# Shifting the wide weight tiles of a two-layer decoder trunk by 64 bytes

## The chip, the core and the metric

The kernel runs on one core of a Trainium2 chip. The metric is the device time of one execution in microseconds. Three runs of the kernel before took 2226.98, 2228.97 and 2231.87 us; the median is 2228.97 us.

## The reference, cut to what matters

Two layers over 512 tokens of width 1024, all in float32. Each layer is a half-step SwiGLU FFN, a token mixer (retention in layer 0, attention with forget gates in layer 1), a second half-step FFN, and a gated per-layer embedding; RMSNorm stands ahead of each, and at the end.

```python
def swiglu(x, w_in, w_out):
    g, u = jnp.split(x @ w_in, 2, axis=-1)
    return (jax.nn.silu(g) * u) @ w_out

for i in range(DEPTH):                       # DEPTH = 2
    h = h + 0.5 * swiglu(rmsnorm(h, nw[0]), ffn_w_in[i, 0], ffn_w_out[i, 0])
    hn = rmsnorm(h, nw[1])
    h = h + (retention(hn, ...) if i == 0 else forgetting_attention(hn, ...))
    h = h + 0.5 * swiglu(rmsnorm(h, nw[2]), ffn_w_in[i, 1], ffn_w_out[i, 1])
    gate = jax.nn.sigmoid(rmsnorm(h, nw[3]) @ ple_w_gate[i])
    h = h + gate * (p[i] @ ple_w_proj[i])
return rmsnorm(h, final_norm_w)
```

`D_MODEL` is 1024 and `D_FF` is 2816.

## The kernel before

**Precision.** Every float32 operand is split into a high part, rounded to the matmul's input format, and a low part, the rest. A product is three matmuls: high by high, high by low, low by high. `mm3` (lines 312 to 314) issues them; line 493 does the same for the FFN's products.

**Layout.** Tokens lie along the free axis. Activations are held in "units" of 128 partitions by 512 columns (pools `ua`, `ub`, `uc`, `ud`, names `unit_a` to `unit_d`). In nearly all matmuls a 128x128 piece of a weight tile is the stationary operand, which a weight load brings into TensorE ahead of each matmul, and a unit is the moving operand: all 512 columns (lines 312 to 314) or one half of 256 columns (lines 493 and 524). In the value projections of the two mixers (lines 678 to 680) it is the other way round: a unit is stationary and 512 columns of a wide weight tile move.

**Weights.** A wide weight tile (name `w8`, shown as `w`) holds the high and the low part of 1024 columns, 8192 bytes in each partition. Three of them rotate in the pool `wpool`. They are filled in the order of a plan, two ahead of use: a DMA on SP's queue into `wraw`, a rounding copy on ScalarE (line 82), and a subtraction on VectorE or GpSimd (line 83), or, for some, a DMA on GpSimd's queue that adds into the tile (line 122).

**FFN.** Of the 22 column blocks of an FFN, two (`plain`, line 524) are computed directly, in 192 matmuls of 256 columns. The other 20 (`start`, `one`, `two`, `three`) use a form of Strassen's method: seven products of 12 matmuls of 256 columns each, line 493. Two of the seven take their weights from the wide tile, 24 matmuls; the other five take them from tiles that the FFN's own pool holds, `s12` and `s34` (sums of weight blocks, shown as `s`) and `a12` (shown as `a`), 60 matmuls. After each of three chunks of blocks the output projection (`out_blocks`) runs 512-column matmuls on wide tiles.

**Where the tiles lie.** Pools are placed one behind the other in each partition. In the built program of before, the units, `wraw`, the three wide tiles of `wpool` and `tmp` begin at 32 modulo 128 bytes. The FFN's `s` and `a` tiles begin at 96 modulo 128, and at 224 modulo 256. In the last stage (`ple` of layer 1, two passes of 256 tokens) five further wide tiles come from a pool `wkept`, which begins at 96 modulo 128; and eight units of `unit_b` hold weights there. All pieces of a tile that a matmul takes lie at multiples of 512 bytes from its beginning, so they share its residue.

**Counts in the program.** Matmuls whose stationary operand lies in `wpool`: 4104 of 512 columns, 2832 of 256 columns (1920 on line 493, 768 on line 524, 144 in the last stage). With a wide tile as the moving operand: 576 of 512 columns. With `s` or `a` stationary: 4800 of 256 columns. With `wkept` stationary: 240 of 256 columns.

**Order.** TensorE's order is the order of the code. The other engines are ordered by the scheduler.

Of the kernel before, what the change touches and what calls it, by code (L numbers as in the profile page):

```python
# [11 lines left out]
F32 = mybir.dt.float32  # L12
# [5 lines left out]
P = 128  # L18
# [169 lines left out]
def trunk(ctx, tc, a):  # L188
    nc = tc.nc
# [6 lines left out]
    uc = ctx.enter_context(tc.tile_pool(name="uc", bufs=4))  # L196
    ud = ctx.enter_context(tc.tile_pool(name="ud", bufs=16))
    wraw = ctx.enter_context(tc.tile_pool(name="wraw", bufs=4))
    wpool = ctx.enter_context(tc.tile_pool(name="wpool", bufs=LOOKAHEAD + 1))
    tmp = ctx.enter_context(tc.tile_pool(name="tmp", bufs=7))  # L200
    stat = ctx.enter_context(tc.tile_pool(name="stat", bufs=1))
    psum = ctx.enter_context(tc.tile_pool(name="psum", bufs=8, space=bass.MemoryType.PSUM))
# [1126 lines left out]
```

## Time and profile before

| | |
|---|---|
| runs | 2226.98, 2228.97, 2231.87 us |
| span of the profiled execution | 2230.5 us |
| granted TensorE clock, mean | 0.987 |
| matmuls | 13525 |
| DMA | 272.33 MB, mean 122 GB/s |

The profile is of one execution whose span, from the first to the last instruction, was 2230.5 us; no other time is given for that execution, and the span lies between the lowest and the highest of the runs. Starts are given in us from the first instruction. The records of matmuls overlap: a matmul's duration covers its way through the array, and the next one starts before it ends. How much time a matmul takes away from the rest is therefore the distance from its start to the next start, called the pitch below. It is read by subtracting two starts and dividing by the count of matmuls between them.

### The profile page before, as it was taken

The page shows a single profiled execution, that of the slowest core. Times are in us where ns is not written, and L with a number is a line of the kernel's source. Part 1 is how long each engine was busy: PE and PEld are TensorE (multiplying, and loading weights), DVE is VectorE, ACT ScalarE, POOL GpSimd, SP SyncE. Part 2 cuts the span into 40 slices and gives each one's busy share as a digit, 9 for nine tenths or more (in the row PEclk, how much of TensorE's full clock was granted, in tenths as well). Part 3 has the DMA queues.
Part 4 walks back from the last instruction along what each step waited for, and adds up shares of the span by engine and source line. Part 5 has one row for each costly group of instructions (what it writes and reads, how often), then busy time and mean ns, then how long its engine had stood idle before and what let it go on. Part 6 is the DMA issues. An engine that isn't in the chain of part 4 may idle for free.

```text
span 2230.5 us, 34455 instructions
## 1 busy us (share of the span) xinstructions
PE 2154.5 (97%) x13525; PEld 1937.5 (87%) x13525; DVE 1447.1 (65%) x2631; ACT 1212.3 (54%) x2037; POOL 450.7 (20%) x352
## 2 busy tenths in 40 slices
PE   7999999999999999999997999999999999999998
PEld 7999997888888798989876989898788888999987
DVE  8686776352542776767746677675675686777764
ACT  7565553433233663735555646364786775555543
POOL 0010003444444010101110001012334200110154
PEclk9999999999999999999998999999999999999999
DMA  5465563232222254746464457373622244655631
GB/s 176 113 163 150 138 161 95 81 99 76 88 83 76 85 137 119 170 133 152 129 151 117 114 136 182 113 167 103 153 91 87 69 116 112 159 158 137 152 104 39
DMA packets 86755, 272.33 MB, mean 122 GB/s; under 512 B 9520, under 2 KB 13104, under 8 KB 86592
## 3 DMA queue, kind: packets, MB, share of 16 engines
q1 hardware_dynamic: 63328, 209.78, 28.7%
q0 software_dynamic: 22032, 59.25, 15.9%
q8 instruction: 106, 1.74, 0.3%
q10 hardware_dynamic: 1232, 1.09, 0.1%
q14 instruction: 57, 0.47, 0.1%
HBM read 267.96 MB, written 2.13 MB: 121 GB/s over the span
## 4 chain that ended last, share of the span: by engine, by line
PE 80%; DVE 7%; ACT 6%; DMA 4%; issue 3%; POOL 0%; SPq 0%; DVEq 0%; ACTq 0%; POOLq 0%
PE bank L493 29%; PE bank L314 14%; PE bank L312 13%; PE bank L313 13%; PE bank L524 3%; DMA wraw<-in_ffn_w_in 3%; PE bank L678 2%; PE bank L679 2%; PE bank L680 2%; DVE w L83 1%; DMA w<-in_ple_gate 1%; DVE sums L151 1%; ACT p L982 1%; ACT w L82 1%; DVE tlo L303 1%
## 5 line engine op out<-in xcount | busy, mean ns | idle before, releaser
L82 ACT CAST w<-wraw 128x1024 fp32r<-128x1024 f32 (+1 forms) x232 | 235.1, 1021 | 431.0 <-PE bank L314 252.6
L314 PE MATMUL bank<-unit_a,w 128*128 128x512 f32 x736 | 288.9, 393 | 12.7 <-DMA w<-in_ple_gate 8.4
L312 PE MATMUL bank<-unit_a,w 128*128 128x512 f32 x736 | 289.8, 394 | 1.9 <-ACT w L82 1.6
L313 PE MATMUL bank<-unit_a,w 128*128 128x512 f32 x736 | 287.9, 391 | 0.2 <-DVE unit_a L303 0.2
L82 ACT CAST s<-sums 128x512 fp32r<-128x512 f32 x320 | 191.2, 617 | 155.3 <-DVE sums L151 106.6
L314 PE MATMUL bank<-unit_d,w 128*128 128x512 f32 (+1 forms) x712 | 268.1, 377 | 4.6 <-DVE w L83 4.6
L312 PE MATMUL bank<-unit_d,w 128*128 128x512 f32 (+1 forms) x712 | 269.2, 378 | 3.2 <-ACT w L82 1.6
L313 PE MATMUL bank<-unit_d,w 128*128 128x512 f32 (+1 forms) x712 | 268.3, 377 | 1.8 <-DVE unit_d L303 1.8
L83 DVE TENSOR_TENSOR s<-sums,s 128x512 fp32r<-128x512 f32 x320 | 213.7, 686 | 81.4 <-ACT s L82 80.4
L83 POOL TENSOR_TENSOR w<-wraw,w 128x1024 fp32r<-128x1024 f32 x83 | 202.6, 2445 | 233.5 <-ACT w L82 223.4
L122 POOL DMA_DIRECT2D a<-in_ffn_w_in x80 | 70.1, 876 | 651.4 <-ACT a L121 444.8
L83 DVE TENSOR_TENSOR w<-wraw,w 128x1024 fp32r<-128x1024 f32 (+1 forms) x149 | 175.8, 1185 | 28.3 <-ACT w L82 27.7
L493 PE MATMUL bank<-unit_b,s 128*128 128x256 f32 x880 | 185.9, 278 | 0.0
L493 PE MATMUL bank<-unit_d,s 128*128 128x256 f32 x1140 | 179.2, 277 | 0.0
L314 PEld LDWEIGHTS bank<-unit_a,w 128*128 128x128 f32 x736 | 138.8, 189 | 45.5 <-DMA w<-in_ple_gate 10.1
L493 PE MATMUL bank<-unit_a,s 128*128 128x256 f32 x1260 | 176.1, 277 | 1.9 <-ACT unit_a L376 1.1
L585 DVE SCALAR_TENSOR_TENSOR tmp<-bank,rows 128x512 f32<-128x512 f32 x96 | 66.0, 689 | 165.3 <-PE bank L314 164.0
L312 PEld LDWEIGHTS bank<-unit_a,w 128*128 128x128 f32 x736 | 139.0, 189 | 32.4 <-ACT w L82 3.5
L313 PEld LDWEIGHTS bank<-unit_a,w 128*128 128x128 f32 x736 | 139.0, 189 | 28.8 <-DVE unit_a L303 0.5
L493 PEld LDWEIGHTS bank<-unit_a,s 128*128 128x128 f32 x1260 | 158.8, 188 | 2.7 <-ACT unit_a L376 1.6
L314 PEld LDWEIGHTS bank<-unit_d,w 128*128 128x128 f32 x712 | 134.4, 189 | 30.5 <-DVE w L83 6.6
L312 PEld LDWEIGHTS bank<-unit_d,w 128*128 128x128 f32 x712 | 134.5, 189 | 30.3 <-ACT w L82 3.3
(270 smaller groups left out, 4801.1 us busy)
## 6 DMA issues: line engine op xcount, KB each, us to landing
wraw<-in_ffn_w_in SPq DMA_DIRECT2D x174, 512.0 KB, 4.3
wraw<-in_ffn_w_out SPq DMA_DIRECT2D x64, 512.0 KB, 4.7
w<-in_ffn_w_in POOLq DMA_DIRECT2D x58, 512.0 KB, 5.5
a<-in_ffn_w_in POOLq DMA_DIRECT2D x80, 256.0 KB, 6.2
wraw<-in_ffn_w_out SPq DMA_DIRECT2D x32, 384.0 KB, 3.7
wraw<-in_ret_qk SPq DMA_DIRECT2D x16, 512.0 KB, 3.5
wraw<-in_ret_v SPq DMA_DIRECT2D x16, 512.0 KB, 3.6
wraw<-in_ret_g SPq DMA_DIRECT2D x16, 512.0 KB, 3.5
```

What stands on the lines that cost most here:

```text
L82: self.nc.scalar.copy(hi, raw)
L83: self.low.tensor_tensor(out=lo, in0=raw, in1=hi.bitcast(F32), op=ALU.subtract)
L122: self.nc.gpsimd.dma_start(out=lo, in_=src, accum_op=ALU.add)
L312: nc.tensor.matmul(out, wh, xh, start=first, stop=False)
L313: nc.tensor.matmul(out, wh, xl, start=False, stop=False)
L314: nc.tensor.matmul(out, wl, xh, start=False, stop=last)
L493: add = lambda w, x, start, stop: nc.tensor.matmul(out, w, x, start=start, stop=stop, skip_group_check=True)
L524: nc.tensor.matmul(o[:, HALVES[t]], x[:, ks], y, start=k == t == q == 0, stop=k == KB - 1 and q == 2, skip_group_check=True,)
L585: nc.vector.scalar_tensor_tensor(out=t1, in0=o, scalar=-0.5, in1=n.r, op0=ALU.mult, op1=ALU.mult)
L678: nc.tensor.matmul(os[t], xh, wh[:, js], start=k == 0, stop=False)
L679: nc.tensor.matmul(os[t], xh, wl[:, js], start=False, stop=False)
L680: nc.tensor.matmul(os[t], xl, wh[:, js], start=False, stop=k == KB - 1)
```

## The change

Two tiles of 128 partitions by 16 float32, 64 bytes in each partition, are allocated: one ahead of `wpool` and one behind it. GpSimd fills each with zeros once, and nothing reads them. The wide tiles then begin at 96 modulo 128. What is allocated behind the second gap is moved by 128 bytes, so `tmp`, the statistics and the pools of the stages keep their residue modulo 128; their residue modulo 256 changes (`s` and `a` from 224 to 96). Everything ahead of `wpool` stays.

```diff
     wraw = ctx.enter_context(tc.tile_pool(name="wraw", bufs=4))
+    nc.gpsimd.memset(ctx.enter_context(tc.tile_pool(name="gap0", bufs=1)).tile([P, 16], F32, name="gap0"), 0.0)
     wpool = ctx.enter_context(tc.tile_pool(name="wpool", bufs=LOOKAHEAD + 1))
+    nc.gpsimd.memset(ctx.enter_context(tc.tile_pool(name="gap1", bufs=1)).tile([P, 16], F32, name="gap1"), 0.0)
     tmp = ctx.enter_context(tc.tile_pool(name="tmp", bufs=7))
```

On GpSimd the program of before begins like this, up to the identity matrix that the transposes use:

```order
L1319 MEMSET const-uint8-127 128x1
L1325 UNCONDITIONAL_BRANCH
masks.py:197 MEMSET ident 128x128
masks.py:199 ISA
masks.py:199 AFFINE_SELECT ident<-ident 128x128
L122 DMA a_434<-in_ffn_w_in 128x512
```

The changed program has the two fills at the same place:

```order
L1321 MEMSET const-uint8-127 128x1
L1327 UNCONDITIONAL_BRANCH
L199 MEMSET gap_81 128x16
L201 MEMSET gap_89 128x16
masks.py:197 MEMSET ident 128x128
masks.py:199 ISA
masks.py:199 AFFINE_SELECT ident<-ident 128x128
L122 DMA a_444<-in_ffn_w_in 128x512
```

Two short instructions more stand ahead of the identity matrix. On the other four queues, TensorE's, VectorE's, ScalarE's and SP's, the instructions and their order are the same as before; only line numbers, buffer numbers and addresses differ.

## The prediction

> **What bounds the kernel now.** I began with the page's busy times and its chain of work that ended last.
>
> ```profile
> PE 2154.5 (97%) x13525; PEld 1937.5 (87%) x13525; DVE 1447.1 (65%) x2631; ACT 1212.3 (54%) x2037; POOL 450.7 (20%) x352
> PE 80%; DVE 7%; ACT 6%; DMA 4%; issue 3%; POOL 0%; SPq 0%; DVEq 0%; ACTq 0%; POOLq 0%
> ```
>
> TensorE (PE) is busy for 97% of the span, and four fifths of the chain are its own matmuls. No other engine is near its limit. The chain in order of time shows an FFN chunk as one piece, and the window view how much room the others have there:
>
> ```profile
> 884.61 77.44 PE bank L493 x672
> ...
> 1027.92 5.29 DMA wraw<-in_ffn_w_in
> ```
> ```profile
> 900.00:960.00 60.00, 60.00 (x523) 60.00 (x523) 48.40 (x88) 44.14 (x77) 9.60 (x11) 1.00 0.76 188
> ```
>
> Columns of the second: PE, PEld, DVE, ACT and POOL busy, granted clock, DMA share, GB/s. Inside a chunk PE has no gap, VectorE is at 48.4/60 = 81% and DMA at 0.76: what changes the pitch of matmuls there changes the time. From 1027.92 on the chain passes through weight loads, and a faster PE would only wait longer.
>
> Nothing but addresses changes, so the question is whether the pitch depends on them. I looked at the order of time of TensorE, where the columns are start, duration, line, operands and count:
>
> ```profile
> 65.10 2.88 PE L493 MATMUL bank<-unit_a,s 128*128 128x256 f32 x24
> 67.82 1.60 PE L493 MATMUL bank<-unit_a,w 128*128 128x256 f32 x12
> 69.26 0.73 PE L493 MATMUL bank<-unit_b,s 128*128 128x256 f32 x5
> ```
>
> 24 matmuls with weights in `s` (96 modulo 128) take 67.82 - 65.10 = 2.72 us, a pitch of **113.3 ns**; 12 with weights in `w` (32) take 1.44 us, **120.0 ns**. Width, line and moving units are the same. The chunk agrees to the last digit: 672 matmuls are 8 blocks of 60 and 24, 480 x 113.3 + 192 x 120.0 = 77.4 us. So weights 64 bytes away from the residue of the moving operand seem to cost 6.7 ns less. Two further views say that this is not all.
>
> First, the 512-column matmuls. The view by tile gives minimum, median and maximum duration, weight loads above matmuls:
>
> ```profile
> L493 PEld LDWEIGHTS bank<-unit_a,s x1260: 186/188/330, 40.2 to 1081.3; 128*128 128x128 f32 x180
> L493 PEld LDWEIGHTS bank<-unit_a,w x540: 187/192/337, 55.9 to 1078.6; 128*128 128x128 f32 x180
> L312 PEld LDWEIGHTS bank<-unit_a,w x736: 186/188/334, 366.2 to 2152.6; 128*128 128x128 f32 x184
> ```
> ```profile
> 1082.91 0.40 PE L312 MATMUL bank<-unit_d,w 128*128 128x512 f32 x1
> ...
> 1084.29 0.39 PE L312 MATMUL bank<-unit_d,w 128*128 128x512 f32 x1
> ...
> 1085.65 0.39 PE L312 MATMUL bank<-unit_d,w 128*128 128x512 f32 x1
> ```
>
> Under 256-column matmuls the loads from `w` are stretched to 192 ns against 188 from `s`; under 512-column ones the loads from the same `w` take 188, as if nothing collided. Their pitch is (1085.65 - 1084.29)/6 = **226.7 ns**, twice 113.3. Right after the change from `s` it is (1084.29 - 1082.91)/6 = 230: there is a stretch of adjustment before the cadence settles.
>
> Second, weights at 96 don't always give 113.3. The window view has a granted clock (the figure behind POOL's) of 0.81 shortly before the first of these rows, and those behind them are of the last stage:
>
> ```profile
> 60.00:61.00 1.00, 1.00 (x9) 1.00 (x9) 0.00 (x0) 0.88 (x1) 0.00 (x0) 0.81 0.00 0
> ```
> ```profile
> 60.85 1.58 PE L493 MATMUL bank<-unit_a,s 128*128 128x256 f32 x12
> 62.26 0.75 PE L493 MATMUL bank<-unit_b,a 128*128 128x256 f32 x5
> ```
> ```profile
> 2176.52 0.28 PE L312 MATMUL bank<-unit_d,w 128*128 128x256 f32 x1
> ...
> 2187.12 0.28 PE L312 MATMUL bank<-unit_d,w 128*128 128x256 f32 x1
> ```
>
> The first 12 run at 1.41/12 = **117.5 ns**. The 90 matmuls between the last two rows have their weights in `wkept`, at 96 as well, and keep 10.60/90 = 117.8 ns to the end. In the FFN the 113.3 comes back only after a product with weights at 32 (the rows from 65.10 follow one). I read this as two cadences at 96: a tight one, which a regular stream keeps but doesn't find by itself, and a loose one, in which a wait leaves it. At 32 a 256-column stream falls into 120.0, and from there passes tightly into 96. After the change no weights of an FFN lie at 32, so nothing there leads back in this way.
>
> **The change part by part.** The sum is made against the profiled span, 2230.5 us, which is 1.5 us (0.07%) over the median 2228.97 of the runs.
>
> *The two fills* are the only new instructions. They stand at the beginning of GpSimd's queue, ahead of the identity matrix, and zero 16 columns each; GpSimd is busy for 450.7 us of the span, and the first matmuls of the FFN need other tiles. Zero. Were that cover gone, a fill can't cost more than the 1.02 us of a GpSimd pass over 256 columns:
>
> ```profile
> L1117 POOL TENSOR_SCALAR hall<-hall,small 128x256 f32<-128x256 f32 x16 | 16.3, 1021 | 13.7 <-ACT acc L425 12.2 <-ACT tmp L428 1.4
> ```
>
> *FFN blocks, 256 columns.* A block has 84 matmuls, now 60 x 113.3 + 24 x 120.0 = 9.68 us. In the tight cadence all 84 take 9.52 us, 0.16 less; in the loose one at 117.5 they take 9.87, 0.19 more, since the 60 that were tight lose 4.2 ns each. Which holds depends on the waits. The third FFN begins with one, and and in the second the chain passes through ScalarE before its last 180 matmuls of line 493, a little over two blocks:
>
> ```profile
> 813.95 0.50 PE L493 MATMUL bank<-unit_b,w 128*128 128x256 f32 x2 [2.28 <-ACT tmp L545]
> ```
> ```profile
> 1059.26 1.04 ACT w L120
> 1060.31 0.95 ACT w L121
> 1062.09 20.98 PE bank L493 x180
> ```
>
> I take it that all four FFNs have such waits at both ends; between them the 512-column stretch, whose loads look undisturbed, should hand on the tight cadence. I take 12 blocks of 20 tight and 8 loose: -1.9 + 1.5 us. The 192 matmuls of the two plain blocks, among waits, go from 120.0 to 117.5: -0.5 us. For four FFNs 4 x (-0.9) = **-3.6 us**; all tight would be 4 x (-3.2 - 1.3) = -18 us, all loose 4 x (3.8 - 0.5) = +13 us.
>
> *512 columns, weights in `w`, 4104 matmuls.* No row shows one at 96 with the moving operand at 32. Bounds: -6.7 ns each, if the gain is per weight load, -27 us; and the nearest row of a 512-column matmul whose operands differ by 64 bytes, in the attention, where the moving `thi`/`tlo` lie at 96 and the weights at 32:
>
> ```profile
> 1625.85 0.40 PE L1012 MATMUL bank<-thi,unit_b 128*128 128x512 f32 x1
> 1626.09 0.40 PE L1013 MATMUL bank<-tlo,unit_b 128*128 128x512 f32 x1
> 1626.32 0.34 PE L1012 MATMUL bank<-thi,unit_b 128*128 128x384 f32 x1
> ```
>
> (1626.32 - 1625.85)/2 = 235 ns, twice 117.5: +8.3 ns each, +34 us. I take **0**, because the load's 188 ns says that this stream has no collision to lose, and it finds its cadence by itself within six matmuls at 1082.91.
>
> *512 columns of `w` moving, 576 matmuls.* They come to the case of the last rows: 0 to +8.3 ns, up to +4.8 us. I take 0, since two matmuls after a switch say little of a long stream.
>
> *The last stage.* 144 matmuls of 256 columns: -2.5 ns each, nothing.
>
> Engines that wait for PE gain or lose with it; buffers come free at the same places in the order. The sum is 2230.5 - 3.6 = 2226.9, **2227 us**.
>
> **The rivals.**
>
> *The loose cadence everywhere (slower).* With no stream at 32 in an FFN, nothing synchronises TensorE after a wait, and at 512 columns too the cadence is the 235 ns of the attention. Price: 4104 x 8.3 = +34, 576 x 8.3 = +5, 4800 x 4.2 = +20, 2832 x -2.5 = -7, together +52 us; some stretches will be tight by luck, or covered by loads as from 1027.92, so +20 to +55, say 2270. For it: the 90 matmuls that never left 117.8. Against it: the 188 ns loads. It decides as soon as the 512-column pitch settles above 227.
>
> *Loose at 256 columns alone (slower).* +20 - 7 + up to 5: +12 to +20 us, 2246.
>
> *Every matmul gains 6.7 ns (faster).* 2832 + 4104 matmuls, with 576 moving: 50 us, less some 7 us hidden by weight loads: 2187 (2180 to 2200). For it: each of the 512-column matmuls has one weight load, like the 256-column ones. Against it: no row has 512 columns below 226, and their loads take 188 ns, so the 226.7 isn't shown to hold a collision.
>
> *The residue modulo 256 decides (slower).* `s` and `a` move from 224 to 96 modulo 256. If their 113.3 came from that, the 4800 would go to 120.0: 4800 x 6.7 = +32 us, 2263. The rows of before can't separate the two.
>
> *Nothing happens.* The pitch difference would come from another property of the tiles. The wide tiles of `wkept`, of the same shape as those at 32, speak against it with 117.8, though weakly. 2230. [...]
>
> **How the numbers follow.** Forecast, tight and loose mixed with 512 columns unchanged: 0.42, its own range 2212 to 2240. Loose everywhere: 0.24. Loose at 256 alone: 0.10. All gain: 0.14. Modulo 256: 0.04. Nothing: 0.06. Under 0.2%, 4.5 us, this kernel's measurement can't tell a difference. Of the forecast's 0.42 I give 0.19 to faster, 0.19 to the same and 0.04 to slower. Faster: 0.19 + 0.14 = 0.33. Same: 0.19 + 0.06 = 0.25. Slower: 0.04 + 0.24 + 0.10 + 0.04 = 0.42: the likeliest case alone is about even, but more of the rivals are slower. The range, 2196 to 2275, leaves out most of "all gain" and the upper part of "loose everywhere", some 0.18.
>
> **What would show it.** The pitch by starts in the profile after: `s` and `w` on line 493 at 113.3 (tight) or near 117.6 (loose), block by block; lines 312 to 314 at 226.7 (mine), 220 (all gain) or 235 (loose); lines 678 to 680 at 227 or 235. The median durations of weight loads from `w` under 256 columns should fall from 192 to 188. I am wrong if 512 columns move away from 226.7, or if the FFN blocks are all of one kind.

## The result, and the profile after

The changed kernel takes 2253.71 us, the median of four runs (2249.75 to 2257.53), against 2228.15 for the kernel before (2226.98 to 2231.87). The ratio is 1.0108, with a 95% interval of 1.0088 to 1.0127: 25.6 us slower. The forecast was 2227; the time lies inside the stated range, in the lower part of what the first rival allowed (20 to 55 us more), and not where the forecast's sum put it.

The page of the changed kernel gives, as before, the busy times and the shares of the chain that ended last:

```profile
PE 2184.7 (97%) x13525; PEld 1942.5 (86%) x13525; DVE 1447.6 (64%) x2631; ACT 1212.8 (54%) x2037; POOL 451.0 (20%) x354
PE 85%; DVE 6%; ACT 4%; issue 2%; DMA 2%; POOL 1%; SPq 0%; ACTq 0%; DVEq 0%; POOLq 0%
```

The span is 2255.7 us, 25.2 more than before. TensorE is busy for 30.2 us more (2184.7 against 2154.5), so it is idle for 5.0 us less: waits of 2.18, 0.42 and 1.88 us, which stood in the last chunk of the second, third and fourth FFN before (at 1062.1, 1487.6 and 2089.1), are gone. The other engines work as long as before, within 0.5 us (VectorE 1447.6 against 1447.1, ScalarE 1212.8 against 1212.3, GpSimd 451.0 against 450.7). The same matmuls come at a slower pitch.

Where? First the 512-column matmuls with weights in `w`, in the order of time (start, duration, line, operands):

```profile
102.09 0.39 PE L314 MATMUL bank<-unit_d,w 128*128 128x512 f32 x1
...
104.19 0.40 PE L314 MATMUL bank<-unit_d,w 128*128 128x512 f32 x1
```

Nine matmuls, three each of lines 314, 315 and 316, lie between these two starts: 2.10/9 = **233.3 ns** against 226.7 before. (A record lasts 0.39 to 0.40 us, and the next begins 0.233 us after it; what the part beyond the pitch is, the rows don't show.) They alternate between 231 and 236 ns, or between 233 and 234, and never settle lower. Over all of them, with waits left out, the mean pitch went from 227.0 to 233.3, and the 4104 distances from start to next start together make +24.3 us. The value projections, where `w` is the moving operand, get slower too, but not all alike:

```profile
400.63 0.39 PE L680 MATMUL bank<-w,unit_a 128*128 128x512 f32 x1
...
403.38 0.39 PE L680 MATMUL bank<-w,unit_a 128*128 128x512 f32 x1
```
```profile
475.13 0.40 PE L680 MATMUL bank<-w,unit_a 128*128 128x512 f32 x1
...
477.93 0.40 PE L680 MATMUL bank<-w,unit_a 128*128 128x512 f32 x1
```

Twelve matmuls take 2.75 us in the first pair, 229 ns each, and 2.80 us in the second, 233.3 ns each. Each value holds for a whole stretch of such matmuls: the first stretch, from 397.9 on, has the lower one, and the next three have the higher one. Over all 576 the mean, waits left out, went from 226.9 to 231.6, which makes +3.0 us.

The chain in order of time shows the full FFN chunks as one piece each:

```profile
126.05 76.17 PE bank L495 x672
...
893.32 79.15 PE bank L495 x672
```

672 matmuls at 113.3 ns are 76.2 us, and at 117.8 they are 79.15. Of the eight full chunks, 672 or 636 matmuls, the first is in the tight cadence of the prediction throughout (113.3), and the other seven are in its loose one (117.8); those of 636 take 74.91 us. Before, each chunk of 672 took 77.44. All 256-column matmuls with a moving unit and weights in `w`, `s` or `a` together make +2.2 us. That is the small rest of larger parts: pitch from `s` and `a` +15.8, pitch from `w` -9.5, waits -4.1. The rest of the program gives back some 4 us, and the sum of all distances is +25.2.

The weight loads, in the view by tile, tell a different story from the pitch:

```profile
L314 PEld LDWEIGHTS bank<-unit_a,w x736: 186/188/337, 368.0 to 2180.7; 128*128 128x128 f32 x184
L495 PEld LDWEIGHTS bank<-unit_a,w x540: 187/188/333, 54.5 to 1089.2; 128*128 128x128 f32 x180
```

The median load from `w` on line 495 fell from 192 to 188 ns, as the prediction said it would. On line 314 it stayed at 188, while the pitch there rose by 6.6 ns.

### The profile page after: what moved, and what is told of

The parts are those of the page before. It is cut to its first block, busy times and chain, and to the rows that moved or that the text cites. A ratio compares the mean times of both kernels' runs of the same rounds, so it can differ in the third digit from the quotient of the medians.

```text
span 2255.7 us, 34457 instructions
## 1 busy us (share of the span) xinstructions
PE 2184.7 (97%) x13525; PEld 1942.5 (86%) x13525; DVE 1447.6 (64%) x2631; ACT 1212.8 (54%) x2037; POOL 451.0 (20%) x354
## 4 chain that ended last, share of the span: by engine, by line
PE 85%; DVE 6%; ACT 4%; issue 2%; DMA 2%; POOL 1%; SPq 0%; ACTq 0%; DVEq 0%; POOLq 0%
PE bank L495 34%; PE bank L316 14%; PE bank L314 14%; PE bank L315 14%; PE bank L526 3%; PE bank L681 2%; PE bank L680 2%; PE bank L682 2%; DMA w<-in_ple_gate 1%; DVE w L83 1%; ACT w L82 1%; DVE sums L151 1%; ACT p L984 1%; DVE s L83 1%; DVE tlo L305 1%
## 5 line engine op out<-in xcount | busy, mean ns | idle before, releaser
L316 PE MATMUL bank<-unit_a,w 128*128 128x512 f32 x736 | 293.4, 399 | 12.5 <-DMA w<-in_ple_gate 8.1
L314 PE MATMUL bank<-unit_a,w 128*128 128x512 f32 x736 | 294.4, 400 | 1.8 <-ACT w L82 1.5
L315 PE MATMUL bank<-unit_a,w 128*128 128x512 f32 x736 | 292.7, 398 | 0.2 <-DVE unit_a L305 0.2
L495 PE MATMUL bank<-unit_d,s 128*128 128x256 f32 x1140 | 184.1, 281 | 0.0
```

The costliest lines, as they stand in the source:

```text
L314: nc.tensor.matmul(out, wh, xh, start=first, stop=False)
L315: nc.tensor.matmul(out, wh, xl, start=False, stop=False)
L316: nc.tensor.matmul(out, wl, xh, start=False, stop=last)
L495: add = lambda w, x, start, stop: nc.tensor.matmul(out, w, x, start=start, stop=stop, skip_group_check=True)
```

## The experiments

In what follows, the **distance** is the address of the stationary operand minus that of the moving one. All experiments but e12, which starts from the changed kernel, are described as edits of the kernel before. Those by gaps add a fill of the given size at the places of the two fills of the change; all products are computed in full.

**Is it the distance, the alignment, or the address of the weights?** Four kernels move the pools as a whole.

```diff
+    nc.gpsimd.memset(ctx.enter_context(tc.tile_pool(name="gapu", bufs=1)).tile([P, 24], F32, name="gapu"), 0.0)
     ua = ctx.enter_context(tc.tile_pool(name="ua", bufs=16))
```

This is e1; the others have fills of the same kind. Sizes in bytes, by the pool that each fill stands ahead of (`tmp` is the pool behind `wpool`):

```
              ua   wpool   tmp
e1_all96      96     -      -
e2_w64         -    32     96
e3_units96    64    64      -
e4_s32         -     -     64
```

> 96 bytes ahead of the units shift them and everything behind them alike: units and wide tiles at 0 modulo 128, s and a at 64. Distances between weights and moving operands are those of the kernel before. Theory 'distance' (only the distance modulo 128 between the stationary and the moving operand counts): every pitch stays (256 columns 113.3 with s, 120.0 with w; 512 columns 226.7), 2228 us, within 5. Theory 'pieces' (6.67 ns is the time of 16 columns, 64 bytes; an operand at 32 modulo 64 touches 17 pieces of 64 bytes where an aligned one touches 16, so 17 x 6.67 = 113.3): 256 columns fall to 106.7 to 113.3 and 512 columns to 213.3 to 220; 7872 x about 7 and 4700 x 7 to 13 ns, so 2115 to 2145 us.

> 32 bytes ahead of the wide tiles and 96 behind: wide tiles at 64 modulo 128, units stay at 32, s and a at 96. Distance of weights to units is 32. Theory 'distance' has no row for 32; if the clash is between equal residues alone, 256 columns of w go from 120.0 to 113-118, and 512 columns leave 226.7 for 233 as at distance 64: about 2250 us. Theory 'pieces': weights aligned to 64, their load touches 8 pieces in place of 9; 512 columns at 220 to 226.7 and 256 columns of w at 113.3, 2190 to 2215 us.

> 64 bytes ahead of the units and 64 ahead of the wide tiles: units at 96 modulo 128, wide tiles at 32, s and a at 96. All distances are turned round: w against units 64, s and a against units 0. Theory 'distance': 512 columns 233.3 (4680 x 6.5 = +30 us), s and a 120.0 (4800 x 6.7 = +32), 256 columns of w at 113 to 118 (2832 x -2 to -7 = -6 to -19): 2270 to 2285 us. Theory 'own address' (the residue of the weights alone counts): all pitches as before, 2228.

> 64 bytes behind the wide tiles alone: units and wide tiles at 32 modulo 128 as in the kernel before, s and a at 32 too. All distances 0. Theory 'distance': 512 columns locked at 226.7 as before, all 256-column matmuls at 120.0: 4800 x 6.7 = +32 us, 2260. Theory 'own tile' (the pitch of s comes from another property of these tiles): 113.3 stays, 2228.

Measured: e1 2230.85 us, ratio 1.0007 (0.9989 to 1.0025); e2 2261.96, e3 2271.02 and e4 2258.37 in one run each, against 2228.17 before. One piece of the chain of each, a full chunk of 480 matmuls from `s` and `a` and 192 from `w`; first e1, then e3, then e4:

```profile
884.62 77.44 PE bank L494 x672
```
```profile
901.43 80.16 PE bank L495 x672
```
```profile
888.01 80.63 PE bank L494 x672
```

With everything shifted alike, e1 repeats the 77.44 of before exactly, so a shift that both operands share changed nothing: "pieces" falls, and with it its time of 16 columns. The 6.67 ns is, in these rows, the difference of 120.0 and 113.3. With the units shifted, `s` is the one at distance 0: 480 x 120.0 + 192 x 117.8 = 80.2. "Own address" falls. With all at distance 0, 672 x 120.0 = 80.6. "Distance" gave e1 and e3 within its ranges, and e4 within 2 us. In e2 the 512-column rows show what a distance of 32 does:

```profile
92.56 0.40 PE L314 MATMUL bank<-unit_d,w 128*128 128x512 f32 x1
...
98.86 0.40 PE L314 MATMUL bank<-unit_d,w 128*128 128x512 f32 x1
```

27 matmuls in 6.30 us: 233.3 ns. Its time is 12 us above what was written for it, since its FFN is loose as well (256 columns from `w`, at distance 32, take 118.3 ns).

**Which part of the change costs?** The pads below let wide tiles begin at different offsets, by what they hold.

```diff
+def wide(pool, off):
+    t = pool.tile([P, 2 * 1024 + 32], F32R, name="w8")
+    return t[:, off : off + 2048].rearrange("p (h c) -> p h c", h=2)
...
-        t = self.pool.tile([P, 2, 1024], F32R, name="w8")
+        t = wide(self.pool, 0)
...
-        pair.t = self.pool.tile([P, 2, 1024], F32R, name="w8")
+        pair.t = wide(self.pool, 16)
```

This is e6; e7 has the offsets 0 and 16 the other way round. e5 has fills alone, 192 bytes ahead of `wpool` and 64 ahead of `tmp`.

> Only the wide tiles of the FFN's Strassen blocks (256 columns, line 493) begin 64 bytes later, at 96 modulo 128; those of the 512-column matmuls, of the plain blocks and of the value projections stay at 32. Theory 'distance with history' (at distance 0, 512 columns lock at 226.7; from that lock a 256-column stream at distance 64 starts in the tight cadence; from an unlocked 512-column stream it may start in the loose one): 512 columns 226.7, full chunks 113.3 throughout, 1920 x 6.7 = 12.8 us less than before: 2213 to 2218. Rival 'without 256-column matmuls at distance 0 the FFN goes loose by itself': full chunks at 117.8 as in the changed kernel, 4800 x 4.4 - 1920 x 2.2 = +17: 2245.

> The other part alone: the wide tiles of the 512-column matmuls, of the value projections and of the plain blocks at 96 modulo 128, those of the Strassen blocks at 32 as before. Theory 'distance': 512 columns unlocked at 233.3, 4104 x 6.25 = +25.6 us and 576 moving x 5 = +3, plain blocks -2 to -5; the Strassen blocks keep 113.3 and 120.0, since the products at distance 0 lead back: 2228 + 24 to 29 = 2252 to 2257. Rival 'the loss of the changed kernel comes from its FFN blocks': under 2240.

> 192 bytes ahead of the wide tiles and 64 behind them: wide tiles at 224 modulo 256 (96 modulo 128, as in the changed kernel), s and a at 224 as in the kernel before (96 in the changed one). Theory 'distance modulo 128': same classes as in the changed kernel, 512 columns at 233.3, 2245 to 2260 us. Rival 'modulo 256' (distance 192 is tight, distance 64 is not): s at 113.3 throughout, and w too; 512 columns open; 2225 or below if they lock.

Measured: e6 2231.22 us, ratio 1.0001 (0.9987 to 1.0016); e7 2255.87, 1.0114 (1.0093 to 1.0135); e5 2248.32, 1.0080 (1.0051 to 1.0109). e7's time fits its 2252 to 2257, but by luck: in its trace the 512-column part is +18.5 us where 28.6 were written, and the FFN, for which a small gain was written, adds 5.4. e6 misses its 2213 to 2218, though its chunks are nearly tight: in its trace the 512-column matmuls take back 8.7 us. (Its profiled execution, 2223.95 us, was one of the fastest of twelve, 7 us under the median; the rest of the miss is open.) In both, the pad of 128 bytes put the middle of the three buffers 128 bytes off modulo 256, so neither separates the parts cleanly. A chunk of e6, and its 512-column rows:

```profile
883.57 76.59 PE bank L498 x672
```
```profile
108.81 0.40 PE L317 MATMUL bank<-unit_d,w 128*128 128x512 f32 x1
...
113.00 0.39 PE L317 MATMUL bank<-unit_d,w 128*128 128x512 f32 x1
...
117.09 0.40 PE L317 MATMUL bank<-unit_d,w 128*128 128x512 f32 x1
```

The 18 matmuls from 108.81 have the middle buffer, at distance 128: 4.19/18 = 232.8 ns. The 18 from 113.00 have one at distance 0: 4.09/18 = 227.2. So **128 is not the modulus** here; with 256 all later runs agree. In e5, at distance 192, 512 columns come to a third value:

```profile
91.68 0.39 PE L314 MATMUL bank<-unit_d,w 128*128 128x512 f32 x1
...
97.86 0.39 PE L314 MATMUL bank<-unit_d,w 128*128 128x512 f32 x1
```

6.18/27 = 228.9 ns. Neither theory written for e5 had that; that its time lies in the 2245 to 2260 of the first is luck, since its 512-column matmuls were to be at 233.3.

**The parts again, with one residue modulo 256 for all three buffers** (pad of 64 columns, and a gap of 128 bytes behind, which puts `s` and `a` at 96 as in the changed kernel).

```diff
-    t = pool.tile([P, 2 * 1024 + 32], F32R, name="w8")
+    t = pool.tile([P, 2 * 1024 + 64], F32R, name="w8")
```

Offsets in columns of 4 bytes:

```
                   Strassen blocks   plain blocks   all other wide tiles
e8_ffn96_clean            16               0                 0
e9_after_512back          16              16                 0
e10_only512                0               0                16
```

> As e6, but with each wide tile padded to 33 x 256 bytes, so that all three buffers have one residue modulo 256: Strassen blocks' wide tiles at 96, all others at 32, s and a at 96 modulo 256. Theory 'distance modulo 256 with history' (distance 0 locks 512 columns at 226.7; distance 128, which every other buffer of e6 had, does not, 231 to 233; after the lock, 256 columns at distance 64 are tight): 512 columns 226.7 as before, full chunks at 113.3, 1920 x 6.7 = 12.8 us less: 2212 to 2219. Rival 'the mixed result of e6 is due to the FFN, not to the buffers at distance 128': 2228 or more.

> The changed kernel with one part undone: the wide tiles of the 512-column matmuls and of the value projections are back at 32 modulo 256; all weights of the FFNs' 256-column matmuls, the plain blocks' too, are at 96, as in the changed kernel. Theory 'distance with history': the changed kernel's +27 us of 512 columns go, and its FFN, which now follows locked 512-column stretches, is tight: like e8, less 768 x 2 to 6.7 = 2 to 5 us for the plain blocks: 2208 to 2217. Rival 'the FFN is loose for lack of products at distance 0': full chunks at 117.8, 2228 + 17 = 2245.

> The 512-column part alone: wide tiles of the 512-column matmuls, of the value projections and of the last stage at 96 modulo 256, those of all FFN products at 32 as in the kernel before, s and a at 96 modulo 256. Theory: 4104 x 6.25 = +25.6 us and 576 x 5 = +3; the Strassen blocks keep 120.0 and 113.3, since products at distance 0 lead back to the tight cadence: 2252 to 2260. Rival 's is tight only at distance 192': s at 117.8, 4800 x 4.4 = +21 more, 2275.

Measured: e8 2233.77 us, ratio 1.0018 (1.0008 to 1.0028); e9 2234.97, 1.0021 (1.0009 to 1.0032); e10 2271.38, 1.0185 (1.0166 to 1.0204). All three miss their main expectation, and e10 comes near the 2275 of its rival. The 512-column half held: in e8 they are back at 227.0 in the mean, in e9 too, and in e10 at 233.3. The FFN half fell. A chunk of e8, then one of e10:

```profile
884.87 79.15 PE bank L499 x672
```
```profile
900.22 79.55 PE bank L501 x672
```

In e8 the chunk is loose throughout (672 x 117.8 = 79.15), though a locked 512-column stretch stands ahead of it. In e10 it is 480 x 117.8 + 192 x 120.0 = 79.6: `s` is loose though every block has products at distance 0. What e8, e9 and e10 share with the changed kernel is the residue of `s` and `a`, 96 modulo 256 where the kernel before has 224. (e6 shares it too, but there a third of the blocks has its `w` at 224.)

**Is it that residue?** e13 moves only it, in the kernel before, by a fill of 128 bytes ahead of `tmp`; e12 puts only it back, in the changed kernel, by a second fill of 192 bytes:

```diff
     wpool = ctx.enter_context(tc.tile_pool(name="wpool", bufs=LOOKAHEAD + 1))
-    nc.gpsimd.memset(ctx.enter_context(tc.tile_pool(name="gap1", bufs=1)).tile([P, 16], F32, name="gap1"), 0.0)
+    nc.gpsimd.memset(ctx.enter_context(tc.tile_pool(name="gap1", bufs=1)).tile([P, 48], F32, name="gap1"), 0.0)
```

> 128 bytes behind the wide tiles alone: units and wide tiles at 32 as in the kernel before, s and a at 96 modulo 256 (in the kernel before 224, which is the same modulo 128). Theory 'distance modulo 256': from a product at distance 0 a 256-column stream goes tight at distance 192 but loose at distance 64 (so far 157 of 157, and 144 of 144 in the run with the units shifted): s at 117.7, 4800 x 4.2 = +20 us: 2246 to 2254. Rival 'modulo 128': nothing moves, 2229. Rival 'at 96 modulo 256 as slow as at 32': s at 120.0, 4800 x 6.7 = +32, 2261.

> The changed kernel with the second gap at 192 bytes in place of 64: wide tiles at 96 modulo 256 as in the changed kernel, s and a at 224 as in the kernel before. Theory 'transitions' (a change from distance 192 to 64 turns loose into tight, the way back keeps either): the full chunks come to 113.3 within a block, 7650 x (116.5 - 114) = 19 us less than the changed kernel; 512 columns stay at 233.3: 2231 to 2240. Rival 'with 512 columns unlocked the FFN stays loose': 2250 to 2260.

Measured: e13 2245.79 us, ratio 1.0067 (1.0043 to 1.0090); e12 2244.02, 1.0062 (1.0039 to 1.0086). A chunk of each, e13 first:

```profile
886.68 79.57 PE bank L494 x672
```
```profile
892.32 76.32 PE bank L495 x672
```

Both times lie outside what was expected, e13's by 0.2 us (2246 to 2254), e12's by 4 (2231 to 2240). In e13 128 bytes behind the wide tiles, which change no residue modulo 128, make the chunk 2.1 us longer than the 77.44 of before: `s` at 117.8. In e12 192 bytes where the change has 64 make the changed kernel's chunk tight: 2.8 us less per chunk. Its median, 9.7 us under the changed kernel's, is less of a gain than the 19 expected. The pitch did what was expected (113.9 in the mean), but half of it came back as waits. The view of what TensorE waited for (total, times, longest) has one row that grew, first the changed kernel, then e12:

```profile
PE bank L495 <- ACT tmp L547: 12.9, 4, 5.6
```
```profile
PE bank L495 <- ACT tmp L547: 22.8, 8, 5.6
```

The page of e12 says the same: PE busy 2165.3 us, 19.4 under the changed kernel, in a span of 2246.3, 9.4 under it. The four new waits, 2.0 to 3.0 us each, stand one in the last chunk of each FFN. There the chain passes through the DMAs that bring the weights (in the second FFN 5.10, 6.41 and 6.74 us, from 1035.56, 1046.76 and 1059.26), as it did from 1027.92 on in the kernel before.

**A version that uses it.** Strassen blocks' wide tiles at 224, `s` and `a` at 96, all others at 32:

```diff
-        pair.t = wide(self.pool, 16)
+        pair.t = wide(self.pool, 48)
```

> Wide tiles of the Strassen blocks at 224 modulo 256 (distance 192), s and a at 96 (distance 64), all other wide tiles at 32 (distance 0), each wide tile padded to 33 x 256 bytes. Theory 'transitions': 512 columns locked at 226.7 as before; every block passes from 192 to 64 and so comes to 113.3: 256 columns 13 to 16 us less than before, as in e6, and without e6's loss of 8.8 us at 512 columns: 2213 to 2218. Rival 'e6 was tight because of its buffers at distance 128 or 192 in turn': loose, 2230 to 2235.

Measured: 2218.46 us, ratio to the kernel before 0.9956 (0.9940 to 0.9972): faster than both, by 10.9 us against before, and 0.5 us above the expected range. The order of time at the start of a chunk, right behind a 512-column stretch, shows how it gets there:

```profile
877.82 0.63 PE L499 MATMUL bank<-unit_b,w 128*128 128x256 f32 x4
...
879.23 0.40 PE L499 MATMUL bank<-unit_b,s 128*128 128x256 f32 x2
...
881.97 0.39 PE L499 MATMUL bank<-unit_b,w 128*128 128x256 f32 x2
...
883.33 0.39 PE L499 MATMUL bank<-unit_b,s 128*128 128x256 f32 x2
```

The first 12, at distance 192, are loose: 1.41/12 = 117.5. The 24 from `s`, at distance 64, find the tight cadence on the way (2.74/24 = 114.2). The next 12 from `w` are tight: 1.36/12 = 113.3. A chunk of 672 takes 76.23 us.

Counting all products of at least 12 like matmuls by the cadence before and after the switch gives this table. Those with waits inside are left out, and the counts are good to a few, because some products stand next to a wait.

```
from                      to distance   cadence after            runs
256 columns, distance 0   192           tight 157 of 157         before
256 columns, distance 0    64           loose 157 of 157         e13
256 columns, distance 0    64           loose 154 of 154         e10
256, 64, loose             64           loose 221 of 222         after
256, 64, tight             64           tight 79 of 80           after
256, distance 128          64           tight 48 of 53           e7
256, 192, loose            64           tight 12 of 15           e12
256, 192, loose            64           tight 17 of 20           e11
256, 64, loose            192           loose 10 of 10           e12
256, 64 or 192, tight     the other     tight 275 of 275         e12
256, 64 or 192, tight     the other     tight 271 of 275         e11
512, distance 0, locked    64 or 192    loose 8 of 8, 8 of 8     e8, e11
512, distance 64           64           tight 2, 4, 7 of 10      after, e12, e3
```

In the changed kernel all weights of the FFN are at distance 64, and a stream there kept the cadence in which it began, the loose one 221 times of 222 and the tight one 79 of 80. A full chunk begins behind a 512-column stretch at distance 64, after which both cadences occur, the tight one 2 times of 10.

## Why the prediction went wrong, step by step

**The bound and the kind of effect: right.** The pitch of TensorE's matmuls was said to change, and nothing else did; the two fills take 0.11 us each, at 0.72 and 0.77 us, and cost nothing that shows. The three cadences of 256 columns (113.3, 117.8 and 120.0) are those of the kernels run here wherever the distance is 0, 64 or 192. The "Nothing happens" rival does not agree with 2253.7 us for a change of addresses alone.

**512 columns, weights in `w`: the step that failed.** The prediction took 0 for 4104 matmuls "because the load's 188 ns says that this stream has no collision to lose", and 0 for the 576 with `w` moving. The runs showed +6.2 ns for each of the 4104, +24.3 us, and +4.7 ns for each of the 576, +3.0 us: together a little more than the whole change in time. The 188 ns did not show what it was taken to show. The lower cadence hung on the addresses as much as that of 256 columns did: at distance 0, and at no other distance tried, 512 columns locked at 226.7; at 64 they took 233.3. The neighbouring row with differing residues, 235 ns in the attention, was the better guide, and it stood in the prediction as the upper bound. The duration of a weight load did not tell the pitch here: its median stayed at 188 ns while the pitch rose from 226.7 to 233.3.

Undone by itself, with the FFN left as in the changed kernel (e9), this part gives back 18.7 us in the medians, and 26.8 between the two profiled executions. Done by itself, over e13 with which it shares `s` and `a`, it costs 25.6 (e10, 2271.38 - 2245.79). Each difference of medians is good to some 5 to 7 us either way by the intervals; the 27 us of the trace lie a little above all three.

**FFN blocks: sign and reason wrong, small by luck.** The term was -3.6 us, 12 of 20 blocks tight; it measured +2.2 for the 256-column matmuls, and all but one of the full chunks were loose. It came out small because a loss of 15.8 us at `s` and `a`, a gain of 9.5 at `w` and 4.1 of waits that went away nearly cancel. "Which holds depends on the waits" does not hold for the full chunks: no wait stands ahead of them or in them. (The wait at 813.95, shown there for the third FFN, is in the second.) Two further statements behind the term fell. One is that the 512-column stretch "should hand on the tight cadence": even from the lock the next 256-column stream was loose, 8 times of 8 in e8 and again in e11, and behind the unlocked stretches of the changed kernel it was tight 2 times of 10. The other is that residues count modulo 128: "modulo 256 decides" was given 0.04. It did count, by another way than that rival's: `s` at 96 is not at 120.0 but stays loose at 117.8, and costs 16.4 us alone (e13; 10 to 20 by its interval). The changed kernel pays less for it, because its `w` in the FFN leaves the 120.0 at the same time: e9, which has both, is 10.8 us under e13.

So the parts are, in medians: `s` and `a` at 96 modulo 256, 2229.4 to 2245.8 (e13); the FFN's `w` at 96 as well, down to 2235.0 (e9); the 512-column tiles, up to 2253.7. The first two make +5.6 us together, within their error of the +2.2 of the trace. The second fill, which looks as if it only restores residues, carries the first of them.

**The rivals.** "Loose everywhere", 2270 with 20 to 55 us of loss, was the nearest: 512 columns left 227, the point from which it was said to decide. It put them at 235, they were at 233.3; it put all FFN blocks loose, the first full chunk was tight. It had 0.24 against the forecast's 0.42. "All gain" fell: no pitch of 512 columns is under 226 in any run.

**Waits.** That a faster PE would only wait longer behind 1027.92 held, and more so than allowed for: in e12 half of the 19 us went there. The prediction did not count the reverse, that a slower PE waits less there: in the changed kernel that gave back 4 us.

What stays open is why the loose cadence and the lock exist. The runs give their conditions, not their mechanism in the array or the memory. Distances other than 0, 32, 64, 128 and 192 bytes, and 224 with `w` moving (e2), were not tried.

## What to carry to other kernels

Where TensorE is the bound, read the pitch of its matmuls by pairs of starts, for each width and each pair of tiles, and compare the addresses of the two operands modulo 256: here one pad cost 1.1% and another placement gained 0.4%. The cadence at one distance was no evidence here for the same tile under another width: at distance 0, 256 columns ran at 120.0 ns, their slowest, and 512 at 226.7, their fastest. And a stream's cadence hung on what ran before it: from a product at distance 0, 256 columns came to 113.3 at distance 192 (157 products of 157) and to 117.8 at distance 64 (157 of 157, e13). So test a new placement in the program itself. The pads moved everything behind them too: `s` and `a` went from 224 to 96 modulo 256, which alone cost 16.4 us (e13). Such a part needs its own run.

## What the runs showed of the hardware that was not expected

- The mean pitch of a steady stream had a few values in these runs, most of them near thirds of 6.67 ns, the difference of 120.0 and 113.3: 113.3, 117.8 and 120.0 are 17, 17 2/3 and 18 times it; 226.7, 228.9 and 233.3 are 34, 34 1/3 and 35 times. The 118.3 of 256 columns at distance 32 (e2) is none of them.
- For 512 columns they followed the distance modulo 256: 226.7 at 0 (the kernel before), 233.3 at 32 (e2) and 64 (the changed kernel), 232.8 at 128 (e6). At 192 there were two values: mostly 228.9 in e5, and 228.9 or 233.3 for whole stretches in the value projections of the changed kernel, where a unit at 32 is stationary and `w` at 96 moves. At 256 columns, distance 0 gave 120.0, the slowest (the kernel before, e4).
- At 256 columns and distances of 64 or 192 the same instructions ran at 113.3 or at 117.8 for whole chunks of 672, by the cadence in which they began: the first full chunk of the changed kernel took 76.17 us and the others of its length 79.15.
